# Thirty-three runs of unread products behind the last product of a two-layer hybrid block

## The chip, the cores and the metric

The kernel runs on one core of one Trainium2 chip. The metric is the device time of one execution in microseconds (us). TensorE multiplies: a product holds one operand still (the stationary one, 128 x 128, put in by a weight load of its own) and streams the other through it (the moving one, up to 512 columns here). VectorE, ScalarE and GpSimd do the element-wise work, and SyncE issues most transfers.

## The reference

Two layers, each of four steps with a layer norm after each: a SwiGLU, a mixer (a gated convolution, a gated linear recurrence and a multi-scale pool), cross attention to a memory of 256 rows, and a second SwiGLU. There are 256 tokens of 1024 features, and everything is float32.

```python
for l in range(DEPTH):
    h = layer_norm(ALPHA * h + 0.5 * swiglu(h, ffn1_gate[l], ffn1_up[l], ffn1_down[l]), ln_g[l, 0], ln_b[l, 0])
    z = h @ w_in[l]
    ...
    mix = jnp.concatenate([y_conv, y_rec, y_pool], axis=-1) @ w_out[l]
    h = layer_norm(ALPHA * h + mix, ln_g[l, 1], ln_b[l, 1])
    h = layer_norm(ALPHA * h + cross_attn(h, mem, ca_q[l], ca_k[l], ca_v[l], ca_o[l]), ln_g[l, 2], ln_b[l, 2])
    h = layer_norm(ALPHA * h + 0.5 * swiglu(h, ffn2_gate[l], ffn2_up[l], ffn2_down[l]), ln_g[l, 3], ln_b[l, 3])
return h
```

## The kernel before, in words

Each float32 operand is split into a rounded part and a remainder (`split`, lines 59 and 60, on ScalarE and VectorE), both in a four-byte type that TensorE takes in one instruction for a product; the profile names it f32 or fp32r. A float32 product then is three: rounded by rounded, rounded by remainder, remainder by rounded.

Two helpers issue nearly all products. `mm_cols` (lines 94 to 101) holds weights still and streams activations: seven products of 512 columns (line 97), eight of 256 (line 99) and one more of 512 (line 100), into one accumulator. `mm_rows` (lines 108 to 111) holds 128 tokens of activations still and streams weights, 512 columns as a rule. The weights arrive in slabs of 1 MB (line 73) that SyncE fetches ahead.

The activations of the running layer lie transposed in `xT`, those of the memory in `mT`. Each is 128 partitions by 8 feature blocks by 2 (rounded, remainder) by 256 tokens, so in one partition 4096 elements lie one behind the other, 512 to a feature block.

Some products of the recurrence aren't split. They work on plain float32, in two instructions for each product. Line 578, in the loop over levels c = 1, 2, 4 to 64, streams `q` in another order than it lies in memory: in two halves, in runs of c elements with c skipped after each run.

The last step, `ffn2` of the second layer, ends in `finish` with `last` set. Token block 0 is finished first. For block 1 the second half of the features is done in two pieces of 256 columns into accumulators of their own (lines 267 to 269). After the last of these products only VectorE works (adding, statistics and normalisation, lines 269 to 291), with one small step on GpSimd (line 284), and SyncE and ScalarE issue the output transfers (line 294). Accumulators come from a pool with four buffers for each of the names `acc` and `dn`.

Of the kernel before, what the change touches and what calls it, by code (L numbers as in the profile page):

```python
# [14 lines left out]
E = mybir.EngineType  # L15
PSUM = bass.MemoryType.PSUM

P = 128
# [783 lines left out]
        pend = ffn(l, "ffn2", 3, pend, last=l == DEPTH - 1)  # L802


# [1 line left out]
_INS = [  # L806
    "x", "mem", "ffn1_gate", "ffn1_up", "ffn1_down", "w_in", "conv_w", "rec_lb", "rec_norm_g", "pool_w",
# [22 lines left out]
```

## Time and profile before

| what | us |
|---|---|
| median of the plain runs (2 runs, 1174.75 to 1174.87) | 1174.81 |
| the profiled execution, its own time | 1176.58 |
| its span, from the first to the last instruction | 1174.8 |

The profile is of one execution. A row of a timeline gives the start in us from the span's beginning, the duration in us, the engine, the line of the kernel, the operation, its output and inputs by the program's names (for a product the moving operand comes first), and the shapes. TensorE's products overlap: the next one starts before the one ahead has left the array, so the time that a product costs is the distance from start to start, and its own duration is longer. A row of a stretch gives the stretch, its length, and for each engine the busy us and in brackets the count.

### The profile page before, as it was taken

The numbers are of one execution on the slowest core, as the hardware profiler recorded it, in microseconds if no ns is written. First come the engines' busy times: TensorE is split into PE (matmuls) and PEld (weight loads), VectorE is DVE, ScalarE is ACT, GpSimd is POOL, SyncE is SP. The second block draws the span as 40 slices with busy tenths as digits, with TensorE's granted clock in tenths as the row PEclk, the third lists the DMA queues.
The fourth block names the chain that finished last, engine by engine and source line by source line (L and its number), as shares of the span: only waits on it lengthen the run. The fifth ranks groups of instructions, "written<-read, shape, count | busy, mean of one in ns | idle before, by whom it ended". The sixth has DMA issues, their size and how long they took to land.

```text
span 1174.8 us, 15745 instructions
## 1 busy us (share of the span) xinstructions
PE 1161.9 (99%) x6219; PEld 1001.2 (85%) x6219; DVE 824.7 (70%) x1194; ACT 595.6 (51%) x873; POOL 40.1 (3%) x80
## 2 busy tenths in 40 slices
PE   8999999999999999999999999999999999999997
PEld 6888888888889888888888888888888888888886
DVE  5766567889787666566677665687998777665665
ACT  6555553626456355455355555446354653554550
POOL 7000000000000000000000000000000000000000
PEclk9999999999999999999999999999999999999999
DMA  8655564644474375655466544655255545655440
GB/s 327 252 193 201 174 221 143 220 140 151 172 244 167 96 247 180 215 198 196 144 215 221 202 168 169 228 187 194 73 209 183 212 144 177 217 179 203 164 171 36
DMA packets 98522, 218.23 MB, mean 186 GB/s; under 512 B 3792, under 2 KB 16368, under 8 KB 98448
## 3 DMA queue, kind: packets, MB, share of 16 engines
q1 hardware_dynamic: 97968, 216.68, 53.2%
q8 instruction: 49, 0.80, 0.3%
q10 hardware_dynamic: 288, 0.39, 0.1%
q14 instruction: 25, 0.20, 0.0%
q0 software_dynamic: 192, 0.15, 0.0%
HBM read 216.15 MB, written 1.05 MB: 185 GB/s over the span
## 4 chain that ended last, share of the span: by engine, by line
PE 97%; DVE 2%; DMA 0%; ACT 0%; issue 0%; SPq 0%; DVEq 0%; ACTq 0%
PE acc L97 29%; PE acc L99 17%; PE dn L111 10%; PE dn L109 10%; PE dn L110 9%; PE acc L109 5%; PE acc L110 5%; PE acc L111 5%; PE acc L100 4%; PE acc L149 1%; PE dn L578 1%; DMA raw<-in_ffn_gate_dram 0%; DVE wlo L60 0%; DVE AT L597 0%; PE dn L621 0%; PE acc L759 0%
## 5 line engine op out<-in xcount | busy, mean ns | idle before, releaser
L60 DVE TENSOR_TENSOR wlo<-raw,whi 128x1024 fp32r<-128x1024 f32 (+1 forms) x396 | 471.1, 1209 | 129.7 <-ACT whi L59 73.6
L59 ACT CAST whi<-raw 128x1024 fp32r<-128x1024 f32 (+1 forms) x396 | 399.7, 1043 | 208.2 <-PE dn L111 140.9
L97 PE MATMUL acc<-xT,whi 128*128 128x512 f32 x1400 | 358.5, 393 | 0.0
L97 PEld LDWEIGHTS acc<-xT,whi 128*128 128x128 f32 x1400 | 262.2, 188 | 50.3
L99 PEld LDWEIGHTS acc<-xT,wlo 128*128 128x128 f32 x1600 | 218.3, 190 | 15.5
L99 PE MATMUL acc<-xT,wlo 128*128 128x256 f32 x1600 | 223.5, 282 | 0.0
L109 PE MATMUL dn<-whi,ah 128*128 128x512 f32 x346 | 135.3, 391 | 0.0
L111 PE MATMUL dn<-whi,al 128*128 128x512 f32 x346 | 134.8, 389 | 0.0
L110 PE MATMUL dn<-wlo,ah 128*128 128x512 f32 x346 | 134.6, 389 | 0.0
L105 DVE TENSOR_TENSOR sg<-acc,sg 128x256 f32<-128x256 f32 x72 | 30.4, 422 | 78.4 <-ACT sg L104 78.4
L100 PE MATMUL acc<-xT,whi 128*128 128x512 f32 x200 | 79.2, 396 | 0.0
L111 PEld LDWEIGHTS dn<-whi,al 128*128 128x128 f32 x346 | 64.9, 188 | 13.7
L110 PEld LDWEIGHTS dn<-wlo,ah 128*128 128x128 f32 x346 | 65.0, 188 | 13.5
L109 PEld LDWEIGHTS dn<-whi,ah 128*128 128x128 f32 x346 | 65.1, 188 | 12.6
L104 ACT COPY sg<-acc 128x256 f32<-128x256 f32 x72 | 26.6, 370 | 94.7 <-PE acc L100 94.7
L109 PE MATMUL acc<-whi,xT 128*128 128x512 f32 x160 | 63.4, 397 | 0.1
L110 PE MATMUL acc<-wlo,xT 128*128 128x512 f32 x160 | 63.0, 393 | 0.0
L111 PE MATMUL acc<-whi,xT 128*128 128x512 f32 x160 | 62.8, 392 | 0.0
L104 ACT COPY up<-acc 128x256 f32<-128x256 f32 x72 | 26.6, 370 | 59.8 <-PE acc L100 59.8
L105 DVE TENSOR_TENSOR up<-acc,up 128x256 f32<-128x256 f32 x72 | 30.3, 421 | 31.8 <-ACT up L104 31.8
L109 PE MATMUL dn<-whi,xT 128*128 128x512 f32 x128 | 50.3, 393 | 0.0
L111 PE MATMUL dn<-whi,xT 128*128 128x512 f32 x128 | 49.9, 390 | 0.0
(202 smaller groups left out, 1236.9 us busy)
## 6 DMA issues: line engine op xcount, KB each, us to landing
raw<-in_ffn_up_dram SPq DMA_DIRECT2D x44, 1024.0 KB, 5.0
raw<-in_ffn_down_dram SPq DMA_DIRECT2D x44, 1024.0 KB, 4.8
raw<-in_ffn_gate_dram SPq DMA_DIRECT2D x42, 1024.0 KB, 5.0
raw<-in_w_in_dram SPq DMA_DIRECT2D x24, 1024.0 KB, 5.0
raw<-in_ca_k_dram SPq DMA_DIRECT2D x8, 1024.0 KB, 4.9
raw<-in_w_out_dram SPq DMA_DIRECT2D x8, 1024.0 KB, 4.8
raw<-in_ca_v_dram SPq DMA_DIRECT2D x8, 1024.0 KB, 5.6
raw<-in_ca_q_dram SPq DMA_DIRECT2D x8, 1024.0 KB, 4.9
```

Source lines behind the costliest of these rows:

```text
L59: nc.scalar.copy(hi, src)
L60: nc.vector.tensor_tensor(lo, src, hi.bitcast(F32), op=ALU.subtract)
L97: nc.tensor.matmul(o, w.at(k, cols)[0], x[:, k], start=k == 0, stop=False)
L99: nc.tensor.matmul(o[:, 0, :], w.at(k, cols)[1], x[:, k, 0, :], start=False, stop=False)
L100: nc.tensor.matmul(o, w.at(NK - 1, cols)[0], x[:, NK - 1], start=False, stop=True)
L104: nc.scalar.copy(dst, view(o[:, 1, :]))
L105: nc.vector.tensor_tensor(dst, view(o[:, 0, :]), dst, op=ALU.add)
L109: nc.tensor.matmul(o, xh, wh, start=start, stop=False)
L110: nc.tensor.matmul(o, xh, wl, start=False, stop=False)
L111: nc.tensor.matmul(o, xl, wh, start=False, stop=stop)
L149: nc.tensor.transpose(pt[:, k, :], src[:, (4 * j + k) * P : (4 * j + k + 1) * P], unit)
L578: nc.tensor.matmul(o[:, hh], kc[:, hh, :], view(qf, hh * P + c, (other - c, 2), (2 * c, a), (1, c)), start=True, stop=True,)
```

## The change

Behind the last line of the model, TensorE gets 580 products that nobody reads. They stand in the order in which they are written. All write one accumulator `o`, each starting and closing its own sum; the stationary operand is 128 columns of `xT`, another feature block each time, and the moving one comes from `mT`. `series` issues 14 products. Its list gives step and count of each dimension of the moving operand, the last one running fastest: `[(2, 512)]` is every second element, `[(1, c), (c, 512 // c)]` jumps by c elements at each column and starts again one further when it has come to the end, `[(1, 256), (0, 2)]` reads each element twice, and `[(0, 2), (1, 256)]` a run of 256 twice. There are 30 calls of `series`. With `at` the stationary operand starts 16 columns further. `columns_of` reads the moving operand in plain order and takes the stationary one from another quarter of each feature block for each c, shifted by 16 or 80 columns for the products of 256: two runs of 64 products, half of 512 and half of 256 columns in groups of eight, and a run of 32 of 256 columns.

```diff
+    x1, m1 = (a.rearrange("p k h s -> p (k h s)") for a in (xT, mT))
+
+    def series(dims, at=0, n=14):
+        ncol = 1
+        for d in dims:
+            ncol *= d[1]
+        reach = sum(abs(d[0]) * (d[1] - 1) for d in dims)
+        back = sum(abs(d[0]) * (d[1] - 1) for d in dims if d[0] < 0)
+        for k in range(n):
+            a, b = 512 * (k % 7) + at, min(512 * (k % 6), 4095 - reach) // 512 * 512 + back
+            x = bass.AP(tensor=m1.tensor, offset=m1.offset + b, ap=[list(m1.ap[0])] + [list(d) for d in dims])
+            nc.tensor.matmul(o[:, 0:ncol], x1[:, a : a + P], x, start=True, stop=True)
+
+    def columns_of(order, off, step=0):
+        for c, k, part in order:
+            a = 512 * (k % 7) + 128 * c + off * part
+            x = m1[:, 512 * (k % 7) : 512 * (k % 7) + 512 - 256 * part]
+            nc.tensor.matmul(o[:, 0 : 512 - 256 * part], x1[:, a : a + P], x, start=True, stop=True)
+
+    with tc.manual_schedule(engines={E.PE}):
+        o = acc((P, 512))
+        series([(1, 512)])
+        series([(1, 256), (256, 2)])
+        series([(-1, 512)])
+        series([(2, 512)])
+        series([(4, 512)])
+        series([(8, 512)])
+        for c in (2, 4, 8, 16, 32, 64, 128):
+            series([(1, c), (c, 512 // c)])
+        for c in (16, 32):
+            series([(c, 512 // c), (-1, c)])
+        series([(1, 256), (0, 2)])
+        series([(1, 128), (0, 4)])
+        series([(0, 2), (1, 256)])
+        series([(0, 32), (1, 16)])
+        series([(0, 16), (1, 32)])
+        series([(0, 8), (1, 64)])
+        series([(0, 4), (1, 128)])
+        series([(32, 16), (1, 32)])
+        series([(48, 32), (1, 16)])
+        series([(1, 480)])
+        series([(1, 384)])
+        series([(1, 320)])
+        series([(1, 128), (128, 2)], at=16)
+        series([(1, 256)], at=16)
+        series([(1, 192)], at=16)
+        for off in (16, 80):
+            columns_of([(c, k, part) for c in range(4) for part in range(2) for k in range(8)], off)
+        columns_of([(c, k, 1) for c in range(4) for k in range(8)], 16)
```

## The prediction

> **What bounds the kernel now.** I read the page first: the head, the busy shares, the granted clock and the chain of work that ended last.
>
> ```profile
> span 1174.8 us, 15745 instructions
> PE 1161.9 (99%) x6219; PEld 1001.2 (85%) x6219; DVE 824.7 (70%) x1194; ACT 595.6 (51%) x873; POOL 40.1 (3%) x80
> PEclk9999999999999999999999999999999999999999
> PE 97%; DVE 2%; DMA 0%; ACT 0%; issue 0%; SPq 0%; DVEq 0%; ACTq 0%
> ```
>
> TensorE is the bound: busy for 1161.9 of 1174.8 us, 97% of the last chain, at a granted clock in the top tenth throughout. Whatever is put on TensorE's queue behind the last useful product can hide only under what still runs after that product. So the second view is the timeline from there, and the third the four stretches of the end, with columns for each engine's busy time and count, then the granted clock, the DMA share and GB/s.
>
> ```profile
> 1145.31 0.40 PE L109 MATMUL dn<-whi,ah 128*128 128x512 f32 x1
> ...
> 1162.79 0.39 PE L111 MATMUL dn<-whi,al 128*128 128x512 f32 x1
> 1163.01 0.28 PE L109 MATMUL acc<-whi,ah 128*128 128x256 f32 x1
> ...
> 1167.21 0.28 PE L111 MATMUL acc<-whi,al 128*128 128x256 f32 x1
> 1167.52 0.42 DVE L269 TENSOR_TENSOR h<-h,acc 128x256 f32<-128x256 f32 x1 [1.27 <-PE acc L111]
> ```
>
> ```profile
> 1145.31:1162.79 17.48, 17.48 (x79) 14.45 (x77) 9.15 (x15) 1.95 (x3) 0.92 (x1) 1.00 0.00 1
> 1163.01:1167.49 4.48, 4.47 (x37) 4.26 (x35) 2.81 (x6) 0.00 (x0) 0.00 (x0) 1.00 0.30 117
> 1167.49:1171.67 4.18, 0.00 (x0) 0.00 (x0) 4.04 (x9) 0.00 (x0) 0.92 (x1) 0.77 0.00 0
> 1171.67:1174.80 3.13, 0.00 (x0) 0.00 (x0) 0.00 (x0) 0.00 (x0) 0.00 (x0) 0.50 0.46 168
> ```
>
> The last product starts at 1167.21 and takes 0.28, so it ends at 1167.49. What follows without TensorE is 4.18 us of VectorE's normalisation and 3.13 us of output transfer and closing: 7.31 us in all, the only cover there is.
>
> **What the change adds.** Built, the program differs on TensorE's queue alone: 580 products stand behind the last old one, each with its own weight load; every other engine keeps its instructions in their order, so no queue is moved past and no transfer is added. By width: 400 of 512 columns (24 series of 14, and 64 in the closing runs), 124 of 256 (two series and 96), 14 each of 480, 384, 320 and 192. The first waits on TensorE's own counter, for a product 18 places before it, done long ago; its accumulator comes from the pool of four, whose last readers are copies (L104, L105) of an earlier stage. I cost that wait at nothing: what covers it is the 18 products in between. Nobody waits for the added products but the end of the program.
>
> **Cost of a product that is read as today's are.** From the rows above: 78 products of 512 columns start from 1145.31 to 1162.79, so 17.48 / 77 = 0.227 us from start to start; 36 of 256 columns from 1163.01 to 1167.21, 4.20 / 35 = 0.120 us. The 256 further columns cost 0.107 us, 0.42 ns a column. By that line 480, 384 and 320 columns cost 0.214, 0.174 and 0.147 us. For 192 it gives 0.093 us; as the weight load doesn't shrink with the columns, I put 0.105 between that and the 0.120 of 256. Sum: 400 x 0.227 = 90.8, 124 x 0.120 = 14.9, 14 x (0.214 + 0.174 + 0.147) = 7.5, 14 x 0.105 = 1.5: together 114.7 us. All of it reads one column after the next.
>
> [...]
>
> **Cost of a product read in another order.** The trace has one such product: line 578 reads its moving operand q in two halves and in runs of 1, 2, 4 and so on elements with as many skipped. These are four-byte products that take two instructions for each 128 columns. Their rows, in the timeline, for runs of 2 (the first) and of 16, 32 and 64:
>
> ```profile
> 249.35 1.07 PE L578 MATMUL dn<-q,kc 128*128 128x128 f32 x8
> ...
> 258.31 1.05 PE L578 MATMUL dn<-q,kc 128*128 128x128 f32 x8
> ...
> 261.31 1.06 PE L578 MATMUL dn<-q,kc 128*128 128x128 f32 x8
> ...
> 264.32 1.05 PE L578 MATMUL dn<-q,kc 128*128 128x128 f32 x8
> ```
>
> ```profile
> L578 PE MATMUL dn<-q,kc x112: 270/275/377, 247.2 to 843.0; 128*128 128x128 f32 x112
> ```
>
> With 0.275 us for the last of each eight, start to start is (1.05 - 0.275) / 7 = 0.111 us for long runs and (1.07 - 0.275) / 7 = 0.114 for runs of two: short runs cost some 3 ns in 111, next to nothing. But this is at 128 columns in 0.111 us, 0.87 ns a column, half the pace of the added kind. So broken reading is shown at half pace only, and only with at least two elements out of any four in a row. [...]
>
> Which value for which series: I sort by how far apart in memory columns that follow each other lie.
> - Neighbours, repeats or two apart: the plain series, both backwards kinds, repeats inside and outside, blocks of 16 at a step of 48, step 2, and (1,2),(2,256), whose inner step is 2. They stay close to the line-578 reads, which cost no more than long runs: 0.227 us.
> - Four or more apart at nearly every column: steps 4 and 8; (1,256),(256,2), which jumps 256 elements to and fro; and (1,c),(c,512/c) for c of 4, 8, 16, 32, 64, 128. That is nine series, 126 products; a tenth, (1,128),(128,2), does the same over 256 columns. No row has them at the faster pace, and the only broken reads are at 0.444 us (0.222 for 256 columns), so I take that: 126 x (0.444 - 0.227) + 14 x (0.222 - 0.120) = 27.3 + 1.4 = 28.7 us.
>
> [...]
>
> The other added edits have one answer: start columns shifted by 16 or 80 in the stationary operand cost nothing, as weight loads today start at any multiple of 128 and lie beside the running product. If loads stopped being hidden, the page's 85% busy on PEld says that they would bind narrow products first; that is the reserve in the 0.105.
>
> **Sum.** The first added product starts one step after the last old one, at 1167.21 + 0.12 = 1167.33. Then 114.7 + 28.7 = 143.4 us, and 0.16 us because the very last takes 0.28 and not a step: TensorE ends at 1310.9. VectorE's 4.18 us and the output transfers lie under this and drop out of the path. What is late next is the closing. Today 3.13 us follow VectorE's end, of which the transfer is this:
>
> ```profile
> DMA to landing us min/median/max: 2.0/2.0/2.0
> ```
>
> So about 1.1 us of closing stay (bounds 0 and 3.1): the span becomes 1312.0 us. The profiled execution took 1176.58 us, 1.8 around its span of 1174.8; the median of the plain runs, 1174.81, lies 1.8 under it and so equals the span. I predict the median, 1312 us (the profiled run 1313.8).
>
> **Rivals.**
> - *No read is slow.* All series run at their plain pace: 1167.33 + 114.7 + 0.16 + 1.1 = 1283 us. For it: line 578 shows short runs nearly free, twice. Against: that was at half the pace and never with one element used out of four. Chance 0.14. [...]
> - *Any broken order is slow.* Beside the ten, step 2, (1,2),(2,256) and the three backwards series pay the half pace: 5 x 14 x 0.217 = 15.2 us more, 1327; with the backwards alone, 9.1 more, 1321. For it: the extra 3 ns of runs of two. Against: its size. Chance 0.17.
> - *Wide steps cost twice as much again*, either because each jump takes longer or because the granted clock falls while the array is fed at half pace. The last two rows of the stretches show it falling to 0.77 and 0.50 as soon as TensorE is idle. Price: 126 x 0.444 + 14 x 0.222 = 59.1 us more, 1371. Against: the page's clock row never dips while products run. Chance 0.12.
> - *Not slower.* Nobody reads the products and all write one accumulator, so only the last could count; if the 579 before it were dropped on the way to the chip, what remains ends at 1167.6, under VectorE's 4.18 us, and the time stays 1175. It decides as long as the added work is under the 7.31 us of cover less the closing, some 6.2 us, or 27 products of 512 columns. Against: in the built program all 580 stand on the queue. Chance 0.02.
>
> **How the numbers follow.** The forecast has the remaining 0.55. Its own range is 1300 to 1318, for some of the ten series paying less, and for the closing's bounds. To hold 8 in 10 the range reaches down to the first rival and up past the second, 1282 to 1329: 0.55 + 0.14 + 0.17 = 0.86; it leaves out 1371 and 1175. A difference of 2%, 23 us here, is about what a measurement can tell; every case but the last lies at least 108 us above 1175. Faster by over 2%: 0; within 2%: 0.02; slower: 0.98.
>
> **What would show it.** In the profile after, the added group's 512-column plain products at 0.227 us a step and the 256 ones at 0.120; nine stretches of 14 products that last near 6.2 us in place of 3.2, and one of 3.1 in place of 1.7; backwards, repeat and block series at 3.2; TensorE from 1167.3 to about 1310.9 without a gap, the output transfers landed by 1174 beneath it, the granted clock at 1.00 to the end, and about 1.1 us of closing. The prediction falls if the nine stretches last 3.2 us or over 7, if the clock dips among them, or if products that read in plain order miss 0.227.

## The result, and the profile after

The changed kernel takes 1313.18 us (median of two runs, 1313.15 to 1313.21), 1.117 times the kernel before, 95% interval 1.1148 to 1.1192. The forecast was 1312. The page of the changed kernel, its head, the busy shares and the chain:

```profile
span 1311.5 us, 16905 instructions
PE 1305.6 (100%) x6799; PEld 1101.8 (84%) x6799; DVE 825.1 (63%) x1194; ACT 595.9 (45%) x873; POOL 41.0 (3%) x80
PE 97%; DVE 2%; DMA 0%; ACT 0%; SPq 0%; issue 0%; ACTq 0%
PE acc L97 26%; PE acc L99 15%; PE acc L816 9%; PE dn L111 9%; PE dn L109 9%; PE dn L110 8%; PE acc L109 4%; PE acc L110 4%; PE acc L111 4%; PE acc L100 4%; PE acc L822 2%; PE acc L149 1%; PE dn L578 1%; DMA raw<-in_ffn_gate_dram 0%; DVE wlo L60 0%; DVE AT L597 0%
```

TensorE is busy for 143.7 us more (1305.6 less 1161.9), and the new lines 816 and 822 are on the chain with 9 and 2%. VectorE and ScalarE do what they did. The timeline at the seam:

```profile
1166.10 0.28 PE L111 MATMUL acc<-whi,al 128*128 128x256 f32 x1
...
1166.22 8.96 PE L816 MATMUL acc<-mT,xT 128*128 128x512 f32 x39
1166.43 0.42 DVE L269 TENSOR_TENSOR h<-h,acc 128x256 f32<-128x256 f32 x1 [1.28 <-PE acc L111]
...
1169.03 1.54 DVE L291 SCALAR_TENSOR_TENSOR h<-h,rs,lnb 128x512 f32<-128x512 f32 x3
```

The added products start one step of 0.12 us after the last old one, without a wait, and VectorE's end lies beneath them. So far all is as forecast. The sum inside isn't. Here are stretches of the changed kernel, each one series of 14 products of line 816 (stretch and length in us, busy us and count of products and of weight loads, granted clock, DMA share, GB/s). A count over 14 takes in neighbours that reach into the stretch.

```profile
1166.22:1169.42 3.20, 3.20 (x14) 2.64 (x15) 1.00 0.00 0
1169.42:1172.45 3.03, 3.03 (x16) 2.65 (x15) 1.00 0.48 173
1172.45:1175.72 3.27, 3.27 (x15) 2.63 (x14) 1.00 0.00 0
1175.72:1182.05 6.33, 6.33 (x15) 2.88 (x14) 1.00 0.00 0
1182.05:1188.49 6.44, 6.44 (x15) 2.91 (x14) 1.00 0.00 0
1188.49:1194.53 6.04, 6.04 (x16) 2.89 (x14) 1.00 0.00 0
1194.53:1200.84 6.31, 6.31 (x15) 2.90 (x14) 1.00 0.01 3
...
1225.48:1232.30 6.82, 6.82 (x15) 2.93 (x14) 1.00 0.00 0
1232.30:1236.29 3.99, 3.99 (x16) 2.70 (x14) 1.00 0.00 0
1236.29:1240.02 3.73, 3.73 (x15) 2.69 (x14) 1.00 0.00 0
```

In order: plain; (1,256),(256,2); backwards; step 2; step 4; step 8; (1,2),(2,256); then, further on, (1,64),(64,8); (1,128),(128,4); and blocks of 16 read backwards. Divided by 14 they cost 0.229, 0.216, 0.234, 0.452, 0.460, 0.431, 0.451, 0.487, 0.285 and 0.266 us a product. The order that jumps 256 elements at each column, forecast at 0.444, is cheaper than the plain one. Step 2, forecast at 0.227, is as dear as step 4.

### The profile page after: what moved, and what is told of

The parts are those of the page before. It is cut to its first block, busy times and chain, and to the rows that moved or that the text cites. A ratio compares the mean times of both kernels' runs of the same rounds, so it can differ in the third digit from the quotient of the medians.

```text
span 1311.5 us, 16905 instructions
## 1 busy us (share of the span) xinstructions
PE 1305.6 (100%) x6799; PEld 1101.8 (84%) x6799; DVE 825.1 (63%) x1194; ACT 595.9 (45%) x873; POOL 41.0 (3%) x80
## 4 chain that ended last, share of the span: by engine, by line
PE 97%; DVE 2%; DMA 0%; ACT 0%; SPq 0%; issue 0%; ACTq 0%
PE acc L97 26%; PE acc L99 15%; PE acc L816 9%; PE dn L111 9%; PE dn L109 9%; PE dn L110 8%; PE acc L109 4%; PE acc L110 4%; PE acc L111 4%; PE acc L100 4%; PE acc L822 2%; PE acc L149 1%; PE dn L578 1%; DMA raw<-in_ffn_gate_dram 0%; DVE wlo L60 0%; DVE AT L597 0%
## 5 line engine op out<-in xcount | busy, mean ns | idle before, releaser
L816 PE MATMUL acc<-mT,xT 128*128 128x512 f32 (+5 forms) x420 | 118.3, 451 | 0.0
L816 PEld LDWEIGHTS acc<-mT,xT 128*128 128x128 f32 x420 | 77.7, 194 | 40.6 <-issue 30.5
L109 PEld LDWEIGHTS dn<-whi,ah 128*128 128x128 f32 x346 | 65.1, 188 | 12.6
L105 DVE TENSOR_TENSOR up<-acc,up 128x256 f32<-128x256 f32 x72 | 30.3, 421 | 31.8 <-ACT up L104 31.8
```

What stands on the lines that cost most here:

```text
L105: nc.vector.tensor_tensor(dst, view(o[:, 0, :]), dst, op=ALU.add)
L109: nc.tensor.matmul(o, xh, wh, start=start, stop=False)
L816: nc.tensor.matmul(o[:, 0:ncol], x1[:, a : a + P], x, start=True, stop=True)
```

## The experiments

There are two groups: kernels that read in other orders behind the last useful product, and then kernels without any added product that use what was found. In the first group each series of 14 stands on source lines of its own, so that the timeline gives it a row; start to start is the distance from one row's start to the next, over 14. Where the next row isn't shown, its start was read from the same timeline. Each kernel with such rows was run once.

**All in plain order.** The changed kernel, with plain reads in `series`:

```diff
-            x = bass.AP(tensor=m1.tensor, offset=m1.offset + b, ap=[list(m1.ap[0])] + [list(d) for d in dims])
+            b = 512 * (k % 6)
+            x = m1[:, b : b + ncol]
```

> All 580 added products in plain order at the same widths, nothing else changed. If the order of reading is the only thing that costs extra, the median falls by what the broken series took beyond 0.227 us a product in the profile after (summed over the series some 26.8 us), to 1286 us, about 1.095 of the kernel before. If part of that excess belongs to the position at the end of the program (code loading, the clock), it stays over 1295.

It took 1284.64 us, 1.0931 of the kernel before (1.0913 to 1.0949). The excess in that expectation was summed wrongly: the series of the profile after, added up again, give 29.6 us and not 26.8, so 1283.6 us should have stood there. In its own profile the first added product starts at 1165.4 us and the last at 1279.9: 114.5 us, where the prediction's plain price gives 114.7 less one step of 0.12, 114.6. So nothing of the cost belongs to the place at the program's end, and the order of reading explains the rest, 144.03 us from first to last start in the changed kernel less 114.47, that is 29.6.

**Pairs and two streams.** 22 series behind the kernel before, of this form:

```diff
+        for k in range(14):
+            nc.tensor.matmul(o[:, 0:512], still(k), moving(k, [(4, 256), (1, 2)], 1), **one)
```

`still` and `moving` take the operands as `series` does; the last number is the start element.

> After the last useful product stand 22 series of 14 products of 512 columns, one source line each; per product, from start to start. Distance theory (the prediction's: only jumps of 4 elements or more cost): (4,256),(1,2) near 0.33 at every start, (2,512) 0.227, (1,256),(d,2) near 0.444 for d of 4 and more. Unit theory (a fetch brings two neighbouring elements that begin at an even place, and a few fetched units are kept): (4,256),(1,2) at starts 0 and 2 is 0.22 and at starts 1 and 3 0.44; (3,256),(1,2) 0.33; (8,128),(1,4) 0.22 at both its starts; two streams 0.216 at any even or odd d; (2,256),(512,2) and (4,256),(2,2) 0.44, since each element is a unit of its own. Form theory (only the innermost step counts, 1 or a count of 2 is free): (4,256),(1,2) 0.22 at all four starts, (2,256),(512,2) 0.216, two streams 0.216 at any d. Bank theory (two fetches go side by side if they are far enough apart): two streams slow at d of 4, 16 and 64, fast from 256 on, and (2,256),(512,2) 0.216.

The timeline of this kernel. Lines 823 to 829 are (4,256),(1,2) at the starts 0 to 3, 831 is (3,256),(1,2), 833 and 835 are (8,128),(1,4) at the starts 0 and 2, 837 is (1,256),(4,2), 845 the same with 255, 859 is (2,256),(512,2), and 861 is step 2.

```profile
1172.84 6.48 PE L823 MATMUL acc<-mT,xT 128*128 128x512 f32 x14
1179.14 6.50 PE L825 MATMUL acc<-mT,xT 128*128 128x512 f32 x14
1185.46 6.50 PE L827 MATMUL acc<-mT,xT 128*128 128x512 f32 x14
1191.77 6.54 PE L829 MATMUL acc<-mT,xT 128*128 128x512 f32 x14
1198.13 4.95 PE L831 MATMUL acc<-mT,xT 128*128 128x512 f32 x14
1202.91 3.44 PE L833 MATMUL acc<-mT,xT 128*128 128x512 f32 x14
1206.19 6.54 PE L835 MATMUL acc<-mT,xT 128*128 128x512 f32 x14
1212.55 3.20 PE L837 MATMUL acc<-mT,xT 128*128 128x512 f32 x14
...
1224.65 3.19 PE L845 MATMUL acc<-mT,xT 128*128 128x512 f32 x14
...
1245.80 3.36 PE L859 MATMUL acc<-mT,xT 128*128 128x512 f32 x14
1249.00 6.51 PE L861 MATMUL acc<-mT,xT 128*128 128x512 f32 x14
```

Every theory that was named loses something. Pairs of neighbours cost 0.45 us at all four starts (1179.14 less 1172.84 is 6.30, over 14), which fells the unit theory and, with its 0.22 for these, the form theory too. Runs of four cost 0.234 when they begin at a multiple of four and 0.454 when they begin two later, so aligned groups of four elements do matter. Two streams are fast at a distance of 4 (0.217) as at 255 (0.216), which fells the bank theory. And (2,256),(512,2) costs 0.228: step 2 is slow in one stream (0.452, line 861) and fast in two.

One rule fits all of these times. It describes the orders that were run; how the columns are fetched no run shows. Take the even and the odd columns separately: an order was fast here if in each half two columns that follow each other lie in one aligned group of four elements. Plain order, 0.229 (line 819): even columns 0, 2 | 4, 6, two to a group. Two streams of step 1, 0.216: 0, 1, 2, 3, four to a group. Two streams of step 2, 0.228 (line 859): 0, 2 | 4, 6. Plain order from one element further: odd columns 2 | 4, 6 | 8, 10, still two to a group, and it measures 0.238 (line 821). One stream of step 2, 0.452: 0 | 4 | 8, one to a group. Pairs, 0.450 to 0.454 at the four starts: 0 | 4 | 8 again. Step 3 in pairs: 0, 3 | 6 | 9 and so on, half of the columns alone in their group, and it measures 0.341, halfway between 0.227 and 0.452.

**More streams.** The same with four to sixteen streams and with steps of 3, 5, 6 and 7.

> 25 series of 14 products, one line each. Unit theory with a few kept units: four streams (1,128),(d,4) all near the 0.283 of the profile after whatever d is, six streams between that and 0.44, eight and sixteen streams 0.43 to 0.49 at any distance, except where the streams overlap closely (d of 4 and 8), where nothing changes for four and eight still miss; steps 3, 5, 6 and 7 at 0.43 to 0.46 like 2, 4 and 8. Bank theory: the cost of four and eight streams changes with d: 130, 144, 66 and 72 well away from 128 and 64. Form theory: innermost counts 4, 6, 8 and 16 each have their price, whatever the distance.

Lines 821 and 827 are four streams 16 and 128 apart, 839 six streams of 84, 845 eight streams 64 apart, 847 eight streams 66 apart, 861 step 3:

```profile
1169.31 3.96 PE L821 MATMUL acc<-mT,xT 128*128 128x512 f32 x14
1173.10 3.99 PE L823 MATMUL acc<-mT,xT 128*128 128x512 f32 x14
...
1180.89 4.13 PE L827 MATMUL acc<-mT,xT 128*128 128x512 f32 x14
...
1204.39 4.24 PE L839 MATMUL acc<-mT,xT 128*128 128x504 f32 x14
...
1218.58 7.02 PE L845 MATMUL acc<-mT,xT 128*128 128x512 f32 x14
1225.42 6.35 PE L847 MATMUL acc<-mT,xT 128*128 128x512 f32 x14
...
1271.10 6.49 PE L861 MATMUL acc<-mT,xT 128*128 128x512 f32 x14
```

Four streams cost 0.271 to 0.283 at every distance tried from 4 to 1024, six 0.291, eight 0.43 to 0.49, and the steps 3, 5, 6 and 7 0.438 to 0.456. With four streams the even columns change between two groups at each step, and an order still costs 0.271 to 0.283, far less than 0.45. With eight streams, four groups to a half, it is 0.43 to 0.49. That each half keeps more than one group, but not four, was the author's guess from these two prices; no run shows what is kept. The distance does shift eight streams (0.488 for 64, 0.441 for 66). The bank theory had said that it would, without a number, and why it does stays open.

**The still operand.** Plain and two-stream orders, with operands fixed, exchanged or taken from the attention's `kTh`.

> 22 series of 14 products, one line each: plain and two-stream orders with the stationary operand and the moving one fixed, moved, exchanged or from another tile. If the 11 to 13 ns by which a plain product exceeds the two-stream one (0.227 against 0.216) come from the weight load and the moving read meeting in memory, they change with which tile the stationary one is in, and with the fixed ones, and the two-stream orders stay at 0.216 in all of them; nested two-stream orders of 256, 128 and 64 columns stay at 0.216 too. If they belong to plain order as such, all plain series are 0.227 and all two-stream ones 0.216 whatever is still. If the 0.216 was an accident of one pair of addresses, the two-stream series from other tiles are 0.227.

Line 823 has both operands fixed, 831 `mT` still and `xT` moving, 835 two streams, 843 two streams of 128 in each half with another still tile, 853 plain at 256 columns, 857 two streams at 256, 861 plain at 128:

```profile
1173.62 3.33 PE L823 MATMUL acc<-mT,xT 128*128 128x512 f32 x14
...
1186.31 3.34 PE L831 MATMUL acc<-xT,mT 128*128 128x512 f32 x14
...
1192.66 3.18 PE L835 MATMUL acc<-mT,xT 128*128 128x512 f32 x14
...
1204.74 3.19 PE L843 MATMUL acc<-xT,kTh 128*128 128x512 f32 x14
...
1218.50 1.84 PE L853 MATMUL acc<-xT,kTh 128*128 128x256 f32 x14
1220.18 1.73 PE L855 MATMUL acc<-mT,xT 128*128 128x256 f32 x14
1221.75 1.73 PE L857 MATMUL acc<-xT,kTh 128*128 128x256 f32 x14
1223.31 1.84 PE L859 MATMUL acc<-mT,xT 128*128 128x256 f32 x14
1224.99 1.68 PE L861 MATMUL acc<-mT,xT 128*128 128x128 f32 x14
```

All settled plain series are 0.227 and all two-stream ones 0.216, whatever is still: the excess belongs to the order. At 256 columns it is 0.120 against 0.112, and 128 columns cost 0.108, hardly less. The kernel before has this too: its line 621 streams 128 columns of `v` in plain order, in plain float32.

```profile
267.19 1.06 PE L621 MATMUL dn<-v,AT 128*128 128x128 f32 x8
```

With 0.275 us for the last of the eight, that is (1.06 - 0.275) / 7 = 0.112 us a product, as much as the 0.111 to 0.114 of line 578's broken reads.

**The rule put to the test.** 16 series chosen for where the rule of even and odd columns and its rivals part.

> 16 series of 14 products of 512 columns behind the kernel before. Two-column theory (even and odd columns are fetched apart, and each half runs at full pace if two of its columns that follow each other lie in one aligned group of four elements): steps 3, 4 and 6 in two streams 512 apart cost 0.34, 0.44 and 0.44, step 2 in two streams 513 apart 0.227; the same four elements of every eight cost 0.45 in the order 0,1,4,5 and 0.22 in the order 0,4,1,5; the order 0,4,2,6 costs 0.227, 0,2,1,3 costs 0.227, and 0,4,1,5,2,6,3,7 0.216. If each half keeps two groups, four streams 129 or 131 apart, whose groups change at different times, fall from 0.27 to 0.22; if not, they stay. Form theory (an innermost count of 2 is free): everything with an innermost 2 is 0.216, steps 3, 4 and 6 and the order 0,1,4,5 too. Group theory (all four columns from one group of four, or two streams): 0,4,2,6 and 0,4,1,5 as slow as 0,1,4,5, near 0.45.

Lines 823 and 825 are steps 3 and 4 in two streams, 833 takes four of every eight elements as 0,1,4,5, 835 the same four as 0,4,1,5, 837 takes 0,4,2,6, and 839 and 841 are four streams 129 and 131 apart:

```profile
1172.61 4.92 PE L823 MATMUL acc<-mT,xT 128*128 128x512 f32 x14
1177.36 6.49 PE L825 MATMUL acc<-mT,xT 128*128 128x512 f32 x14
...
1196.23 6.48 PE L833 MATMUL acc<-mT,xT 128*128 128x512 f32 x14
1202.53 3.40 PE L835 MATMUL acc<-mT,xT 128*128 128x512 f32 x14
1205.77 3.38 PE L837 MATMUL acc<-mT,xT 128*128 128x512 f32 x14
1208.99 3.45 PE L839 MATMUL acc<-mT,xT 128*128 128x512 f32 x14
1212.28 3.43 PE L841 MATMUL acc<-mT,xT 128*128 128x512 f32 x14
```

0.339, 0.451, 0.450, 0.231, 0.230 and 0.235 us. The same four elements cost half when their order puts 0 and 1 on even columns and 4 and 5 on odd ones; the form and group theories fall here. The other four orders to which the rule gave a number came out as well: step 6 in two streams 0.450, step 2 in two streams 513 apart 0.229, 0,2,1,3 0.232, and 0,4,1,5,2,6,3,7 0.216. Four streams fall from 0.27 to 0.235 at 129 and 0.233 at 131 (line 841), where the two groups of a half change at different times. The expectation had 0.22 there for halves that keep two groups, and no change for others; 0.235 lies nearer the first. Two results stand outside the rule: eight streams 65 apart rise to 0.50, and step 2 in four streams costs 0.332, though there too each half reads two groups in turn. The rule has no number for either, so what a half keeps is not settled.

**Used in the kernel before.** Three kernels without added products. In the first, `mm_rows` reads its 512 weight columns in two streams, and whoever reads that accumulator puts the columns back in order:

```diff
+    def two(a):
+        return a.rearrange("p (t j) -> p j t", t=2)
+    def apart(a):
+        return a.rearrange("p (t j) -> p t j", t=2)
+    def back(o):
+        return o.rearrange("p (j t) -> p t j", t=2)
...
+        if wh.shape[-1] == 512:
+            wh, wl = two(wh), two(wl)
...
-                        h[i][:, c], h[i][:, c], ALPHA / scale, y[i][n], op0=ALU.mult, op1=ALU.add
+                        apart(h[i][:, c]), apart(h[i][:, c]), ALPHA / scale, back(y[i][n]), op0=ALU.mult, op1=ALU.add
```

> Not the added products but the kernel before, with the 512-column products of mm_rows reading their moving weights in two streams 256 apart, and the readers of those accumulators putting the columns back. 2094 products by 0.011 us are 23 us: 1152 us, 0.980 of the kernel before, if VectorE and ScalarE read the accumulators at a step of two as fast, or with room to spare. If such reads are slower and someone waits for them, the gain is eaten: 1165 to 1180.

1155.55 us, 0.9818 of the kernel before (0.9802 to 0.9835). In the second, `mm_cols` reads its activations in two streams of 128 in each half, and the same is done in `add` and `add_forward`:

```diff
+    def both_two(a):
+        return a.rearrange("p h (t j) -> p h j t", t=2)
...
-            nc.tensor.matmul(o, w.at(k, cols)[0], x[:, k], start=k == 0, stop=False)
+            nc.tensor.matmul(o, w.at(k, cols)[0], both_two(x[:, k]), start=k == 0, stop=False)
...
-            nc.tensor.matmul(o[:, 0, :], w.at(k, cols)[1], x[:, k, 0, :], start=False, stop=False)
+            nc.tensor.matmul(o[:, 0, :], w.at(k, cols)[1], two(x[:, k, 0, :]), start=False, stop=False)
```

> The kernel before with the products of mm_cols reading their activations in two streams of 128 in each half. 1728 products of 512 columns by 0.013 and 1728 of 256 by 0.008 us are 36 us: 1139 us, 0.970 of the kernel before. Here the readers of the accumulators (576 copies and additions) follow each group of 16 products closely, so a slower read at a step of two would show first here: then 1150 to 1180.

1144.39 us, 0.9728 (0.9713 to 0.9742). The third has both edits.

> Both edits: the two gains add, as they are on different products of one engine that is busy nearly all the time: 1174.8 - 23 - 36 = 1116 us, 0.950 of the kernel before; the shares of VectorE and ScalarE rise. If another bound comes near (the weight load at some 0.111 us a product, or VectorE's splitting of the weights), less than the sum: 1125 to 1140.

1121.55 us, 0.9534 (0.952 to 0.9548): a version 4.7% faster than the kernel before. Its head, the chain, one of its groups (line 119 is line 105 of before) and two products of its timeline (lines 125 and 126 are 109 and 110 of before):

```profile
span 1119.0 us, 15740 instructions
PE 1105.0 (99%) x6219; PEld 991.6 (89%) x6219; DVE 821.5 (73%) x1194; ACT 593.0 (53%) x873; POOL 40.5 (4%) x80
PE 91%; DVE 6%; issue 1%; DMA 0%; ACT 0%; SPq 0%; DVEq 0%; ACTq 0%
L119 DVE TENSOR_TENSOR sg<-acc,sg 128x256 f32<-128x256 f32 x72 | 30.4, 422 | 68.4 <-ACT sg L118 68.4
```

```profile
1090.38 0.38 PE L125 MATMUL dn<-whi,ah 128*128 128x512 f32 x1
...
1091.89 0.38 PE L126 MATMUL dn<-wlo,ah 128*128 128x512 f32 x1
```

Seven steps in 1.51 us are 0.216 each. The addition that reads the accumulator at a step of two takes 422 ns as in the kernel before (`sg` of line 105), which this row of before shows:

```profile
L105 DVE TENSOR_TENSOR sg<-acc,sg 128x256 f32<-128x256 f32 x72 | 30.4, 422 | 78.4 <-ACT sg L104 78.4
```

ScalarE's copies from the accumulator take 371 ns against 370. So these readers pay nothing. The gains came a little short of the expectation (20.6, 31.8 and 54.6 us by the medians against 1176.19, where 23, 36 and 59 were expected). VectorE's part of the chain grew from 2 to 6%, but TensorE's idle time grew by 1.1 us alone (1119.0 less 1105.0 against 1174.8 less 1161.9), so waiting explains only part of the shortfall.

## Why the prediction was right in the sum, and where not

- *TensorE is the bound and the cover is 7.31 us:* right; the added work starts one step behind the old and nothing else is on the path.
- *Plain products:* right to 0.1 us in 114.6, by the kernel with all reads in plain order. Start columns shifted by 16 or 80 cost nothing, as forecast: the 160 products of `columns_of` (line 822), 96 of them shifted, start from 1284.4 to 1310.3 in 25.9 us, where the plain prices give 64 x 0.227 + 96 x 0.120 = 26.0 less one step of 0.12, so 25.9 too. 192 columns took 0.110 where 0.105 stood.
- *Which broken orders are slow:* this step failed. It sorted by how far apart columns that follow each other lie. The runs show that columns must be compared with the ones two before them: the same four elements cost 0.450 us in the order 0,1,4,5 and 0.231 in the order 0,4,1,5. Of the ten series priced at the half pace, seven were near the half pace or slower (0.431 to 0.487): steps 4 and 8, and (1,c),(c,512/c) for c of 4 to 64. The two-stream ones weren't (0.216 and, at 256 columns, 0.111), and (1,128),(128,4) paid 0.285. Together these ten took 52.5 us where 59.1 was forecast. Step 2 and (1,2),(2,256), priced at 0.227, paid the half pace: 12.6 where 6.4 stood. Two errors of about 6 us cancelled, and that the total came out so close is luck.
- *Nothing under 0.227 at 512 columns:* wrong too. No order was priced below the pace of plain reading, and two streams run at 0.216.
- *The half pace itself:* right in size; 0.444 was forecast as four times the 0.111 of line 578, and 0.431 to 0.460 measured for single steps. The reason given for taking it, that the trace showed no broken read at a faster pace, was no mechanism, and the agreement is luck. Line 578 streams 128 columns, and plain reads of 128 columns cost as much (0.112 in line 621 of the kernel before, 0.108 in line 861 of the still-operand kernel). Its 0.87 ns a column is what these narrow products cost in either order, and says nothing of broken reading. For the same reason its runs of two, nearly free there, could not show that step 2 is slow at 512 columns.
- *Backwards and short blocks:* near plain, but not equal: 0.234 backwards, 0.266 in backwards blocks of 16. With the rest of this group it came to 1.0 us over the forecast. The rule of even and odd columns doesn't explain the 0.266, and it stays open.
- *The end:* 1.0 us of closing (1311.5 less 1310.5) where 1.1 stood. The first added product came 1.1 us earlier than in the profile of before, which fits that execution having been a long one (1176.58 against a median of 1174.81). For the same reason the step "the median equals the span" was wrong: the changed kernel's plain runs lie 1.7 above its span. These two cancel in part.
- *The rivals:* none of the whole ones came. Half of "any broken order is slow" did, for step 2, and half of "no read is slow", for two streams. The clock stayed at 1.00. Of the signs named against the prediction one came: of the nine stretches that were to last 6.2 us, that of the two streams lasted 3.0 and that of (1,128),(128,4) 4.0.

Taken column by column, a rule of two columns to each aligned group of four elements fails both ways: step 2 has two in each group and costs 0.452, the 256-element jump has no two in a row and costs 0.216. Taken for even and odd columns apart it holds in all one-stream and two-stream orders of step 1 or more that were run: 0.216 to 0.242 us with two or more to a group, 0.431 to 0.460 with one, and 0.339 and 0.341 for the two orders of step 3 that have both.

## What to carry to other kernels

A total that comes out right can hide two wrong terms: price a group of unlike operations so that each one can be checked by itself in the profile. For moving operands of this four-byte type, try to arrange that among the even columns, and likewise among the odd ones, each aligned group of four elements serves at least two columns in succession: the one-stream and two-stream orders of step 1 or more that did so here cost 0.216 to 0.242 us at 512 columns, and a single stream of step 2 doubled the time of a product (0.452 against 0.227). Reading two runs alternately, and putting the columns back where the accumulator is read, was 5% faster per product of 512 columns than plain order here (0.216 against 0.227) and cost the readers nothing (422 ns both ways for VectorE, 371 against 370 for ScalarE).

## What the runs showed of the hardware that was not expected

- Two alternating streams are faster than one plain stream: 0.216 against 0.227 us at 512 columns, at distances from 4 to 2048 elements (0.216 to 0.217), and 0.112 against 0.120 at 256 columns. Why the plain order pays 0.011 us was not settled; it isn't the place of the still operand (0.226 to 0.229 in all eight plain series of 512 columns with other operands).
- At 512 columns the slowest orders with eight and sixteen streams cost 0.49 to 0.53 us, more than any single step did (0.431 to 0.460).
- VectorE and ScalarE read the accumulators at a step of two as fast as in order (422 ns both ways, and 371 against 370).
- After a change of width or of order the first plain products of 512 columns take mostly 0.23 to 0.24 us and settle at 0.227 after some six. This too is left open.
